# First norm's scale row spread by two products with ones, and another order of the first tiles, weights, mLSTM and FFN steps

## The chip, the cores and the metric

The kernel runs on one core of one Trainium2 chip. The metric is the time of one execution on the device, in microseconds (us). The profiler also records one execution: when each instruction began and how long it took on TensorE (PE, with PEld for its weight loads), VectorE (DVE), ScalarE (ACT), GpSimd (POOL) and SyncE (SP), what each waited for, what the 16 DMA engines moved, and the TensorE clock that was granted (1.00 is 2.4 GHz, 0.50 is 1.2 GHz).

## The reference

A trunk of two layers on 512 positions of width 1024, in float32. Layer 0 mixes with a chunked mLSTM, layer 1 with stick-breaking attention; each layer then cross-attends into 256 memory tokens and applies a SwiGLU FFN of inner width 2816. Every sub-layer is normalised before and after.

```
mem_n = rms_norm(mem, mem_norm_gain)
for layer in range(DEPTH):
    g = norm_gains[layer]
    hn = rms_norm(x, g[0])                        # g[0] of layer 0: the first norm's scale row
    y = mlstm_mixer(hn, ...) if layer % 2 == 0 else stick_breaking_mixer(hn, ...)
    x = x + rms_norm(y, g[1])
    y = memory_cross_attention(rms_norm(x, g[2]), mem_n, ...)
    x = x + rms_norm(y, g[3])
    y = swiglu_ffn(rms_norm(x, g[4]), ...)
    x = x + rms_norm(y, g[5])

# mlstm_mixer: proj = h @ w_in is split into q, k, v, output gate o and the head gates;
# per head scores with decay, hs = rms_norm(numerator / denominator), out = hs * sigmoid(o), out @ w_out
```

## The kernel before

**Numbers and products.** Each float32 operand of a product is kept as a high part (`hi`, rounded to fp32r) and a low part (`lo`, the rest). `split` makes them: a cast (`copy`, on ACT or DVE) and a subtraction on DVE. A product is three matmuls, lo·hi, hi·lo and hi·hi (`mm3` and `product`, issued at line 510). Transposes of activations (`flip`, line 524) also run on PE; four of them fill a bank of 512 columns.

**Weights** come in blocks of 128 x 1024 elements (512 KB), issued by SP (`dma`, line 418). Most projections use `seven` (line 643), which makes seven block products where eight would be needed: it loads three blocks, adds a fourth onto two of them with accumulating loads from POOL (`gather`, line 423), and forms its last sum `w10 + t2` on DVE, or with a third `gather` from SBUF to SBUF if its number in starting order is in `BY_DMA`.

**The start.** `warm` (line 770) runs 18 products of zeros on PE. SP loads the first 128 positions `xin[0]` in two halves, then the scale row of the first norm, broadcast to 128 partitions (`g0`, a 512 KB write), then by turns a pair of weight blocks for half of v (`w_tm`) and the next 128 positions. `arrive(t)` normalises tile t (sum of squares on ACT, logarithm and exponential on ACT, a few small steps on DVE, then one scaling by `g0` on DVE, line 468), flips it and splits it into `hi` and `lo`. The loop `for d in range(NT)` in `mlstm` brings tile d and weight d together and multiplies what has become possible. `constants` fills masks on POOL.

**mLSTM.** `MORDER` says in what order steps are made: `q`, `r` project q and k of two heads each, `+` is `sum_blocks` (sums of activation blocks that `seven` needs), `V` the other half of v, `s` scores, `h` heads, `o` and `P` the output gate. Then `proj_out` multiplies with `w_out` (eight blocks; here "out rows", three matmuls of 512 columns each per k), `boundary` does the norms, and `memory` normalises the 256 memory tokens and flips them.

**What sets the order.** Each operation is handed to `Plan.op` with an estimated duration and a rank (for PE the sum of PE time so far, moved by `later` and `sooner`). `lay_out` goes through time once and gives each engine, whenever it is free, the operation of least rank that can start and finds buffers; `LEAD` ranks the loads of some weights earlier, `SCARCE` keeps spare buffers from operations far ahead. The result is one fixed list for each engine, and every engine works its list strictly in order, so one late operation holds all behind it. Buffers are slots (44 of 4 KB and more, called `big`; 8 of 2 KB, `half`; 8 banks, `ps`).

Of the kernel before, what the change touches and what calls it, by code (L numbers as in the profile page):

```python
# [8 lines left out]
F32 = mybir.dt.float32  # L9
R = mybir.dt.float32r  # L10
# [6 lines left out]
P = 128  # L17
D = 1024
S = 512
NT = S // P  # L20
# [8 lines left out]
GROUPS = ((0, 8), (8, 16), (16, 22))  # L29
UNITS = ((0, '+', 2, 4, 6, 2, 6, 4, 2, 6, 8, 4, 8, (0, 1), (0, 0), 8, (0, 0), 10, (0, 0), (0, 1), 12, 14, 10, 14, (0, 1), 12, 10, 16, 14, 16, 12, 18, 16, 20, 18, 20, 20, (1, 0), (1, 1), (1, 1), 18, (1, 1), (1, 0), (1, 0)), (0, 2, 4, '+', 2, 6, 2, 4, 6, 8, 4, 6, (0, 1), 8, 8, (0, 0), (0, 1), (0, 0), (0, 1), (0, 0), 10, 10, 10, 12, 14, 16, 12, 18, 12, 14, 16, 14, 16, 18, 20, 20, 20, (1, 1), 18, (1, 0), (1, 0), (1, 1), (1, 0), (1, 1)))  # L30

# [346 lines left out]
class Trunk:  # L378
# [35 lines left out]

    def dma(self, eng, out, in_, ns=1400):
        q = {"SP": "sync", "POOL": "gpsimd", "ACT": "scalar"}[eng]
        cost = {"SP": 500, "POOL": 1040, "ACT": 60}[eng]
        self.plan.op(eng, cost, lambda nc: getattr(nc, q).dma_start(ap(out), ap(in_)), [in_], [out], load=ns)

# [65 lines left out]

    def memset(self, out, val):
        self.plan.op("POOL", 60 + 0.3 * out.free, lambda nc: nc.gpsimd.memset(ap(out), val), [], [out])

# [8 lines left out]

    def mms(self, items, **kw):

        ns, reads, writes = 0.0, [], []  # L500
# [11 lines left out]
        self.plan.op("PE", ns, fn, reads, writes)  # L512

# [250 lines left out]

    def gain(self, row, eng="POOL"):
        g = self.plan.buf("gain", (P, D))
        self.dma(eng, g, row.broadcast_to([P, D]))
        return g

    def warm(self, n):  # L770

        z, ps = self.half(S, dt=R), self.bank()
        self.memset(z.bitcast(F32), 0.0)
        self.mms([(ps, z[:, 0:P], z, True, True)] * n)
        self.plan.pe = 0.0

# [100 lines left out]
    def constants(self):  # L877
        self.eps = self.const(P, 1)
        self.memset(self.eps, EPS)
        raw = self.half(P)  # L880
# [4 lines left out]
        self.ident = self.ident_r.bitcast(F32)  # L885

        self.above = self.half(NT, P, dt=R)
        self.strict = self.const(P, 2, P, dt=R)
        for m, op, fill in ((self.above, ALU.is_ge, BIG), (self.strict, ALU.is_gt, -BIG)):
            raw = self.half(*m.idx.shape)  # L890
            self.memset(raw, 0.0)
# [4 lines left out]
        self.memset(raw, -1.0)  # L896
        self.select(raw[:, 0], ALU.is_ge, 0.0, 0, [[-1, P]], 1)
# [4 lines left out]
        raw = self.half(MLH, P)  # L902
        self.memset(raw, 0.0)
        for base in (0, -32):
# [5 lines left out]
    def mlstm(self, h, arrive, w_in, b_gate, head_gain, w_out, filler, finish):  # L910
        QK = MLH * MLK
# [11 lines left out]
        banks, ws = [], []  # L923
        for d in range(NT):
            with self.later(START * d):
                arrive(d)
                ws.append(self.w_tm(w_in, 2 * d, 2 * QK))
                banks.append(self.bank(2, 256))
                banks[d].buf.chained = True
                for t, u in [(t, d) for t in range(d)] + [(d, u) for u in range(d + 1)]:  # L930
# [3 lines left out]
        for t in range(NT):  # L934
            evac_v(0, t, banks[t])
        wg, bias = self.gate_weights(w_in[:, 2 * QK + 2 * D :], b_gate)
# [55 lines left out]

        hg = self.gain(head_gain)
        hs = [self.big(D) for _ in range(NT)]
# [544 lines left out]
def trunk_kernel(tc, x, mem, mem_norm_gain, norm_gains, ml_w_in, ml_b_gate, ml_head_gain, ml_w_out,  # L1539
# [117 lines left out]
```

## Time and profile before

| | |
|---|---|
| median of 3 runs | 1494.31 us (1491.07 to 1494.38) |
| the profiled execution | 1494.13 us, of which the span from first to last instruction is 1492.3 us |
| busy: PE, PEld, DVE, ACT, POOL | 1473.7, 1375.7, 1212.9, 863.2, 142.5 us |
| DMA | 191.00 MB, 128 GB/s over the span |
| granted TensorE clock, mean | 0.996 |

The span is nearly all PE time, so what counts is where PE stands still or runs below its usual pace. [...]

### The profile page before, as it was taken

Reading aid. Unit: us, or ns where it says so; the run is one execution under the profiler, and the core shown is the slowest. Engines: PE = TensorE matmul, PEld = TensorE weight load, DVE = VectorE, ACT = ScalarE, POOL = GpSimd, SP = SyncE. Lnnn points to the kernel's source line nnn. Section 1 sums busy time; section 2 is a strip of 40 time slices with the busy share of each in tenths; the row PEclk is TensorE's granted clock in tenths of the full one; section 3 lists DMA queues with packets and bytes.
Section 4 is the critical chain, followed back from the end, with each engine's and each line's share of the span. In section 5 each row is a group of like instructions: output and inputs, shape, how many; then the busy total and the mean of one; then the engine's idle time right before and its main releaser. Section 6 shows DMA issues by size and latency. Waiting matters only on the chain. (4 is left out here: it accounts for less than half of the span.)

```text
span 1492.3 us, 26099 instructions
## 1 busy us (share of the span) xinstructions
PE 1473.7 (99%) x10364; PEld 1375.7 (92%) x10364; DVE 1212.9 (81%) x1920; ACT 863.2 (58%) x1532; POOL 142.5 (10%) x180
## 2 busy tenths in 40 slices
PE   8999999999999999999999999999999999999998
PEld 6999889998999999998889888888988999999996
DVE  7979879886887786898868998879787969768985
ACT  7658655663654454654459896656556645444532
POOL 2100100100111111110100010001000111110110
PEclk9999999999999999999999999999999999999999
DMA  7446646532655566684400136244515563854651
GB/s 240 90 84 152 213 142 211 100 114 85 182 101 129 122 134 141 135 208 152 127 29 29 57 98 208 76 147 126 166 57 162 109 126 71 203 123 86 155 170 57
DMA packets 166955, 191.00 MB, mean 128 GB/s; under 512 B 6960, under 2 KB 140592, under 8 KB 166832
## 3 DMA queue, kind: packets, MB, share of 16 engines
q1 hardware_dynamic: 119776, 121.68, 25.5%
q0 software_dynamic: 47056, 67.64, 23.3%
q8 instruction: 82, 1.34, 0.4%
q14 instruction: 41, 0.34, 0.1%
HBM read 176.72 MB, written 10.49 MB: 125 GB/s over the span
## 5 line engine op out<-in xcount | busy, mean ns | idle before, releaser
L510 PE MATMUL ps<-big,big 128*128 128x256 f32 (+2 forms) x9712 | 1409.4, 306 | 7.4 <-ACT sm L434 2.7
L510 PEld LDWEIGHTS ps<-big,big 128*128 128x128 f32 x9712 | 1293.2, 189 | 91.5 <-ACT sm L434 2.9
L456 DVE TENSOR_TENSOR big<-big,big 128x1024 fp32r<-128x1024 f32 (+1 forms) x515 | 606.8, 1211 | 47.8 <-ACT big L441 27.4
L441 ACT CAST big<-big 128x1024 fp32r<-128x1024 f32 x388 | 393.4, 1044 | 154.8 <-DMA big<-in_ffn_w_gate_up_dram 48.2
L434 ACT ACTIVATE half<-ps 128x512 f32<-128x512 f32 (+4 forms) x185 | 92.7, 525 | 109.4 <-PE ps L510 100.0
L456 DVE TENSOR_TENSOR big<-ps,big 128x512 fp32r<-128x512 f32 (+3 forms) x188 | 109.5, 603 | 37.2 <-ACT big L441 23.9
L441 ACT CAST big<-ps 128x512 fp32r<-128x512 f32 (+2 forms) x166 | 81.4, 514 | 97.7 <-PE ps L510 61.2
L441 ACT COPY half<-ps 128x512 f32<-128x512 f32 (+2 forms) x102 | 59.6, 585 | 123.4 <-PE ps L510 116.1
L456 DVE TENSOR_TENSOR big<-half,big 128x512 fp32r<-128x512 f32 (+4 forms) x150 | 82.7, 577 | 7.2 <-ACT big L434 5.6
L434 ACT ACTIVATE half<-big 128x512 bf16<-128x512 f32 (+1 forms) x63 | 41.9, 666 | 72.6 <-DVE big L456 44.8
L423 POOL DMA_DIRECT2D big<-in_ffn_w_gate_up_dram x40 | 51.3, 1291 | 317.6 <-DVE big L456 193.1
L468 DVE SCALAR_TENSOR_TENSOR half<-ps,half 128x512 f32<-128x512 f32 (+2 forms) x74 | 46.8, 645 | 36.1 <-ACT half L441 20.9
L456 DVE TENSOR_TENSOR half<-ps,half 128x512 f32<-128x512 f32 (+2 forms) x78 | 46.8, 631 | 15.8 <-PE ps L510 14.3
L441 ACT CAST big<-half 128x512 fp32r<-128x512 f32 (+3 forms) x105 | 50.1, 521 | 13.4 <-DVE half L456 8.5
L456 DVE TENSOR_TENSOR big<-ps,gain 128x512 f32<-128x512 f32 x32 | 22.0, 687 | 35.6 <-ACT half L434 35.1
L434 ACT ACTIVATE half<-half 128x512 f32<-128x512 f32 (+2 forms) x74 | 40.5, 586 | 14.8 <-DVE half L456 14.5
L434 ACT ACTIVATE big<-ps 128x512 fp32r<-128x512 f32 (+2 forms) x66 | 38.4, 593 | 12.7 <-PE ps L510 9.3
L524 PE MATMUL ps<-const,big 128*128 128x128 f32 (+1 forms) x314 | 43.0, 275 | 2.0 <-DVE big L468 2.0
L524 PEld LDWEIGHTS ps<-const,big 128*128 128x128 f32 (+1 forms) x314 | 37.0, 143 | 7.8 <-issue 2.6
L510 PE MATMUL ps<-big,const 128*128 128x256 f32 (+3 forms) x224 | 41.0, 320 | 0.0
L510 PEld LDWEIGHTS ps<-big,const 128*128 128x128 f32 x224 | 36.4, 189 | 4.4
L461 DVE TENSOR_SCALAR sm<-sm,sm 128x1 f32<-128x1 f32 x99 | 23.8, 242 | 18.6 <-ACT half L434 10.0
(86 smaller groups left out, 616.0 us busy)
## 6 DMA issues: line engine op xcount, KB each, us to landing
big<-in_ffn_w_gate_up_dram SPq DMA_DIRECT2D x68, 512.0 KB, 5.2
big<-in_ffn_w_gate_up_dram POOLq DMA_DIRECT2D x40, 512.0 KB, 6.1
big<-in_ffn_w_down_dram SPq DMA_DIRECT2D x36, 512.0 KB, 5.8
big<-in_xa_w_kv_dram SPq DMA_DIRECT2D x32, 512.0 KB, 5.5
big<-in_sb_w_qkv_dram SPq DMA_DIRECT2D x24, 512.0 KB, 4.0
big<-in_ml_w_in_dram SPq DMA_DIRECT2D x19, 512.0 KB, 7.1
dr<-big POOLq DMA_DIRECT2D x16, 512.0 KB, 5.8
big<-in_xa_w_o_dram SPq DMA_DIRECT2D x16, 512.0 KB, 6.6
```

What stands on the lines that cost most here:

```text
L423: "POOL", 1040, lambda nc: nc.gpsimd.dma_start(ap(out), ap(in_), accum_op=ALU.add), [in_, out], [out], load=ns
L434: nc.scalar.activation(ap(out), ap(in_), func, scale=ap(scale), **kw)
L441: "ACT", 0.833 * n + (60 if psum else 95), lambda nc: nc.scalar.copy(ap(out), ap(in_)), [in_], [out],
L456: self._dve(out, [a, b], lambda nc: getattr(nc, q).tensor_tensor(out=ap(out), in0=ap(a), in1=ap(b), op=op), eng)
L461: nc.vector.tensor_scalar(out=ap(out), in0=ap(a), scalar1=ap(s1), scalar2=ap(s2), op0=op0, **kw)
L468: lambda nc: nc.vector.scalar_tensor_tensor(out=ap(out), in0=ap(a), scalar=ap(s), in1=ap(b), op0=op0, op1=op1),
L510: nc.tensor.matmul(ap(out), lhsT=ap(a), rhs=ap(b), start=start, stop=stop, **kw)
L524: nc.tensor.transpose(ap(out), ap(in_), ap(ident))
```

## The change

The scale row of the first norm is no longer loaded broadcast. `first_gain` loads the row once into one partition (from POOL), and two products with a row of ones spread it over 128 partitions; two copies bring it to `g0`. Zero products stand around them: 5 of 512 columns first, then 34 of 256 columns, which the planner may put wherever PE would wait. They are float32 products, unlike all others, where the row itself is multiplied. The order of the first tiles and weights becomes x, w, w, w, x, x, w, x. The masks are filled after the first v bank is done, and the mLSTM's head gain is loaded after all v banks. `MORDER` puts the first `q` ahead of `+`. `BY_DMA` changes; its number 39 is higher than any `seven` reaches, so q, V, r, P of the mLSTM and two of layer 0's FFN use the third gather, where before it was V, o, P and one of layer 0's FFN. Two FFN steps of layer 0 change places in `UNITS`, twice.

```diff
-MORDER = '+qqVqrsVVrrssosoohhPhhPP'
-START = 1250
+MORDER = 'q+VqqsrVVrrssosoohhPhhPP'
+START = 0
+SOON = 0
-BY_DMA = (1, 3, 4, 18)
+BY_DMA = (0, 1, 2, 4, 15, 20, 39)
-WARM = 18
+ARRIVE = 'xwwwxxwx'
+COLD, WARM = 5, 34
-LEAD = {'stick': 14000, 'ffn': 0, 'cross': 0, 'ml_out': 4500, 'sb_out': 2000, 'xa_out': 2000}
-SCARCE = {'ps': (4000, 0), 'big': (7000, 5), 'half': (4000, 2)}
+LEAD = {'stick': 14000, 'ffn': 0, 'cross': 0, 'ml_out': 3500, 'sb_out': 2000, 'xa_out': 2500}
+SCARCE = {'ps': (4000, 0), 'big': (7000, 5), 'half': (2000, 2)}
+    def first_gain(self, row):
+        src, ones, z, idle = self.big(D), self.half(P), self.half(S, dt=R), self.bank()
+        self.dma("POOL", src[0:1], row, 100)
+        self.memset(z.bitcast(F32), 0.0, "DVE")
+        self.memset(ones[0:1], 1.0, "DVE")
+        plan = self.plan
+        for _ in range(COLD):
+            self.mms([(idle, z[:, 0:P], z, True, True)], ns=430)
+            plan.pe = 0.0
+        g = self.plan.buf("gain", (P, D))
+        for c in (slice(0, 512), slice(512, D)):
+            ps = self.bank()
+            self.mms([(ps, ones[0:1], src[0:1, c], True, True)], ns=1300)
+            plan.pe = 0.0
+            self.copy(g[:, c], ps)
+        plan.pe = 0.0
+        with self.later(3000):
+            for _ in range(WARM):
+                self.mms([(idle[:, 0:256], z[:, 0:P], z[:, 0:256], True, True)])
+                plan.pe = 0.0
+        return g
-        for d in range(NT):
-            with self.later(START * d):
-                arrive(d)
-                ws.append(self.w_tm(w_in, 2 * d, 2 * QK))
+        for i, what in enumerate(ARRIVE):
+            with self.later(START * i), self.sooner(SOON * (len(ARRIVE) - 1 - i)):
+                if what == "x":
+                    arrive(len(banks))
+                else:
+                    ws.append(self.w_tm(w_in, 2 * len(ws), 2 * QK))
+        self.masks(banks[0])
-        hg = self.gain(head_gain)
+        hg = self.gain(head_gain, behind=banks)
-    k.warm(WARM)
+    g0 = k.first_gain(norm_gains[0, 0:1])
-    with k.sooner(3000):
-        g0 = k.gain(norm_gains[0, 0:1], "SP")
```

What the lists show at the places that matter. First SP, at the very start: `big_68` and `big_108` are the first two tiles of x before, `big_70` and `big_96` in the changed kernel; `in_ml_w_in` are weight blocks. Before:

```order
L418 DMA big_68<-in_x_dram 128x512 x2
L418 DMA gain_103<-in_norm_gains_dram 128x1024
L418 DMA big_106<-in_ml_w_in_dram 128x2x512
L418 DMA big_108<-in_x_dram 128x1024
L418 DMA big_111<-in_ml_w_in_dram 128x2x512
L418 DMA big_113<-in_x_dram 128x1024
```

and in the changed kernel:

```order
L422 DMA big_70<-in_x_dram 128x512 x2
L422 DMA big_80<-in_ml_w_in_dram 128x2x512
L422 DMA big_92<-in_ml_w_in_dram 128x2x512
L422 DMA big_96<-in_x_dram 128x1024
L422 DMA big_101<-in_ml_w_in_dram 128x2x512
L422 DMA big_108<-in_x_dram 128x1024
```

The broadcast scale row is gone from SP's list, and two weight blocks stand ahead of the second tile.

PE at the start before: `half_72` holds zeros, L524 are flips of a tile of x.

```order
L510 MATMUL ps_78<-half_72 128x512 x18
L524 MATMUL ps_166<-const_101,big_68 128x128 x4
L524 MATMUL ps_192<-const_101,big_68 128x128 x4
L510 MATMUL ps_235<-big_173,big_222 128x512
L510 MATMUL ps_235<-big_209,big_190 128x512
```

and in the changed kernel, where `half_68` holds zeros, `half_74` the ones, `big_72` the row:

```order
L516 MATMUL ps_76<-half_68 128x512 x5
L516 MATMUL ps_76<-half_68 128x256 x8
L516 MATMUL ps_117<-big_72,half_74 128x512
L516 MATMUL ps_156<-big_72,half_74 128x512
L516 MATMUL ps_76<-half_68 128x256 x10
L530 MATMUL ps_194<-const_98,big_70 128x128 x4
L516 MATMUL ps_76<-half_68 128x256 x12
L530 MATMUL ps_221<-const_98,big_70 128x128 x4
L516 MATMUL ps_76<-half_68 128x256
L516 MATMUL ps_231<-big_163,big_217 128x512
```

The two halves of the first tile are now flipped apart, and both, like everything behind, wait for the two products of the row. After these rows come, for the first tile, 11 more matmuls with w0 and w1, 3 zero products, 6 with w2, the flips of tile 1, 6 with w3, then tile 1's own.

ACT late in the mLSTM, where `P` waits for its last gathered block. Before (`big_1604` is that block, `ps_2084` a flipped piece of the heads, `sm_2119` the norm of the last heads):

```order
L441 CAST big_2071<-big_1881 128x1024
L434 ACTIVATE half_2089,sm_2006<-ps_2055 128x256
L441 CAST big_2108<-big_1604 128x1024
L434 ACTIVATE sm_2119<-sm_2112,const_66 128x4
L441 CAST big_2135<-ps_2084 128x2x128
L434 ACTIVATE sm_2119<-sm_2119 128x4
```

and in the changed kernel (`big_1613`, `ps_2113`, `sm_2148`):

```order
L438 ACTIVATE half_2118,sm_2035<-ps_2084 128x256
L445 CAST big_2135<-ps_2113 128x2x128
L445 CAST big_2139<-ps_2113 128x2x128
L438 ACTIVATE sm_2148<-sm_2141,const_66 128x4
L438 ACTIVATE sm_2148<-sm_2148 128x4
L445 CAST big_2165<-big_1613 128x1024
L445 CAST big_2171<-big_1918 128x1024
```

The cast of the gathered block now stands behind the norm of the last heads instead of ahead of it. On PE two more groups of four flips stand ahead of that block's product, and between it and the flips of the memory tokens there are 39 matmuls of 512 columns where there were 57. Behind the mLSTM's output projection PE's list is the same but for two small moves in layer 0's FFN and one in layer 1's cross-attention.

## Rows read from the trace of the kernel before

**Rows 1.** The page's first line.

```profile
span 1492.3 us, 26099 instructions
```

**Rows 2.** Busy time of each engine by stretch, granted clock, DMA share, GB/s.

```profile
4.50:9.00 4.50, 2.80 (x12) 1.95 (x11) 2.21 (x6) 2.19 (x6) 4.50 (x23) 1.00 0.98 315
11.30:18.10 6.80, 4.84 (x16) 4.09 (x17) 5.20 (x10) 5.96 (x14) 0.00 (x0) 0.50 1.07 375
60.00:160.00 100.00, 100.00 (x820) 98.95 (x819) 87.37 (x188) 70.69 (x155) 15.40 (x17) 1.00 0.53 115
160.00:166.00 6.00, 3.26 (x23) 2.83 (x22) 2.15 (x7) 3.23 (x7) 0.00 (x0) 0.91 1.06 388
200.00:620.00 420.00, 420.00 (x3140) 400.23 (x3139) 338.63 (x478) 231.61 (x378) 38.07 (x33) 1.00 0.53 129
```

**Rows 3.** Timeline of PE, first 23 us: start, length, count, idle before.

```profile
1.56 5.74 PE L510 MATMUL ps<-half 128*128 128x512 f32 x18 [1.56 <-POOL half L487]
9.30 1.23 PE L524 MATMUL ps<-const,big 128*128 128x128 f32 x8 [2.00 <-DVE big L468]
...
15.95 1.91 PE L524 MATMUL ps<-const,big 128*128 128x128 f32 x8
17.51 4.70 PE L510 MATMUL ps<-big,big 128*128 128x512 f32 x18
22.06 1.03 PE L524 MATMUL ps<-const,big 128*128 128x128 f32 x8
```

**Rows 4.** Timeline of DVE and ACT, first norm and first weight.

```profile
5.89 0.59 DVE L468 SCALAR_TENSOR_TENSOR sm<-sm,sm 128x1 f32<-128x1 f32 x1
...
7.95 1.87 DVE L468 SCALAR_TENSOR_TENSOR big<-big,sm,gain 128x512 f32<-128x512 f32 x2 [1.47 <-DMA gain<-in_norm_gains_dram]
...
9.28 1.05 ACT L441 CAST big<-big 128x1024 fp32r<-128x1024 f32 x1 [2.17 <-DMA big<-in_ml_w_in_dram]
```

**Rows 5.** DMA issues: count, KB each, median us from issue to landing.

```profile
big<-in_x_dram SPq DMA_DIRECT2D x2, 256.0 KB, 2.9
gain<-in_norm_gains_dram SPq DMA_DIRECT2D x1, 512.0 KB, 6.1
...
sm<-in_ml_b_gate_dram POOLq DMA_DIRECT2D x2, 0.0 KB, 7.0
```

**Rows 6.** Groups by shape, whole span: busy us, mean ns of one.

```profile
L456 DVE TENSOR_TENSOR big<-big,big 128x1024 fp32r<-128x1024 f32 x419 | 500.9, 1219 | 37.0 <-ACT big L441 26.8 <-PE ps L510 7.0 <-issue 1.1
...
L456 DVE TENSOR_TENSOR big<-ps,big 128x512 fp32r<-128x512 f32 x98 | 64.8, 685 | 16.5 <-ACT big L441 15.8
...
L468 DVE SCALAR_TENSOR_TENSOR big<-big,sm,gain 128x512 f32<-128x512 f32 x42 | 30.3, 759 | 2.1 <-DMA gain<-in_norm_gains_dram 1.5
...
L441 ACT CAST big<-big 128x1024 fp32r<-128x1024 f32 x382 | 389.8, 1050 | 154.4 <-DMA big<-in_ffn_w_gate_up_dram 48.2 <-DVE big L456 31.6 <-PE ps L510 28.6
...
L441 ACT CAST big<-ps 128x512 fp32r<-128x512 f32 x94 | 53.1, 589 | 70.6 <-PE ps L510 40.8 <-PE ps L524 24.8 <-issue 3.3
```

**Rows 7.** Timeline of SP, ACT and PE around the stop at 162 us.

```profile
142.56 15.42 SPq L418 DMA_DIRECT2D big<-in_ml_w_out_dram  x8
...
162.77 1.04 ACT L441 CAST big<-big 128x1024 fp32r<-128x1024 f32 x1 [3.82 <-DMA big<-in_ml_w_in_dram]
...
163.86 0.38 PE L510 MATMUL ps<-big,big 128*128 128x256 f32 x1 [1.86 <-ACT big L441]
165.12 4.42 PE L510 MATMUL ps<-big,big 128*128 128x256 f32 x23 [0.88 <-DVE big L456]
```

**Rows 8.** Timeline of DVE and PE at the flips of the memory tokens.

```profile
188.38 1.27 DVE L468 SCALAR_TENSOR_TENSOR big<-big,sm,gain 128x1024 f32<-128x1024 f32 x1
...
189.70 1.27 DVE L468 SCALAR_TENSOR_TENSOR big<-big,sm,gain 128x1024 f32<-128x1024 f32 x1
...
181.85 9.28 PE L510 MATMUL ps<-big,big 128*128 128x512 f32 x39
190.97 1.04 PE L524 MATMUL ps<-const,big 128*128 128x128 f32 x8
```

More of the change, by code (lines that the diff above doesn't have):

```diff
@@ L412, in sooner, with dma @@
         self.plan.lead = old
-    def dma(self, eng, out, in_, ns=1400):
+    def dma(self, eng, out, in_, ns=1400, behind=()):
         q = {"SP": "sync", "POOL": "gpsimd", "ACT": "scalar"}[eng]
         cost = {"SP": 500, "POOL": 1040, "ACT": 60}[eng]
-        self.plan.op(eng, cost, lambda nc: getattr(nc, q).dma_start(ap(out), ap(in_)), [in_], [out], load=ns)
+        self.plan.op(eng, cost, lambda nc: getattr(nc, q).dma_start(ap(out), ap(in_)), [in_, *behind], [out], load=ns)
     def gather(self, out, in_, ns=2800):
@@ L484, in vcopy, with memset @@
         self._dve(out, [a], lambda nc: nc.vector.tensor_copy(ap(out), ap(a)), fast=True)
-    def memset(self, out, val):
-        self.plan.op("POOL", 60 + 0.3 * out.free, lambda nc: nc.gpsimd.memset(ap(out), val), [], [out])
+    def memset(self, out, val, eng="POOL", behind=()):
+        q = {"DVE": "vector", "POOL": "gpsimd"}[eng]
+        self.plan.op(eng, 60 + 0.3 * out.free, lambda nc: getattr(nc, q).memset(ap(out), val), list(behind), [out])
     def select(self, out, op, fill, base, pattern, cm):
@@ L496, in select, with mms @@
         )
-    def mms(self, items, **kw):
-        ns, reads, writes = 0.0, [], []
+    def mms(self, items, ns=None, **kw):
+        given, ns, reads, writes = ns, 0.0, [], []
         for out, a, b, _, _ in items:
@@ L763, in rest, with gain @@
         return b[:, 0:1], b[:, 1:2]
-    def gain(self, row, eng="POOL"):
+    def gain(self, row, behind=()):
         g = self.plan.buf("gain", (P, D))
-        self.dma(eng, g, row.broadcast_to([P, D]))
+        self.dma("POOL", g, row.broadcast_to([P, D]), behind=behind)
         return g
[L770 to L775, printed above, removed]
+    def first_gain(self, row):
[19 more added lines that the diff above has]
+        return g
     def prenorm(self, out, x, g, steps=False):
@@ L885, in constants, with masks @@
         self.ident = self.ident_r.bitcast(F32)
+    def masks(self, behind):
         self.above = self.half(NT, P, dt=R)
@@ L890, in constants @@
             raw = self.half(*m.idx.shape)
-            self.memset(raw, 0.0)
+            self.memset(raw, 0.0, behind=[behind])
             self.select(raw, op, fill, 0, [[0, m.idx.shape[0]], [1, P]], -1)
@@ L895, in constants @@
         raw = self.half(2, P)
-        self.memset(raw, -1.0)
+        self.memset(raw, -1.0, behind=[behind])
         self.select(raw[:, 0], ALU.is_ge, 0.0, 0, [[-1, P]], 1)
@@ L902, in constants @@
         raw = self.half(MLH, P)
-        self.memset(raw, 0.0)
+        self.memset(raw, 0.0, behind=[behind])
         for base in (0, -32):
@@ L923, in mlstm @@
         banks, ws = [], []
[L924 to L930 removed]
+        for i, what in enumerate(ARRIVE):
+            with self.later(START * i), self.sooner(SOON * (len(ARRIVE) - 1 - i)):
+                if what == "x":
+                    arrive(len(banks))
+                    banks.append(self.bank(2, 256))
+                    banks[-1].buf.chained = True
+                    new = [(len(banks) - 1, u) for u in range(len(ws))]
+                else:
+                    ws.append(self.w_tm(w_in, 2 * len(ws), 2 * QK))
+                    new = [(t, len(ws) - 1) for t in range(len(banks))]
+                for t, u in new:
                     for k in (0, 1):
@@ L933, in mlstm @@
                         self.mm3(banks[t], h.tile(t, kk), ws[u][:, k], kk == 0, kk == KD - 1)
-        for t in range(NT):
-            evac_v(0, t, banks[t])
+                    if u == NT - 1:
+                        evac_v(0, t, banks[t])
+        self.masks(banks[0])
         wg, bias = self.gate_weights(w_in[:, 2 * QK + 2 * D :], b_gate)
```

4 lines of the change are left out of this document (2 added, 2 removed).

## The prediction

> **What bounds the kernel now.** I read the stretches first, then PE's timeline where PE stands still. The profiled execution took 1494.1 us, 1.8 more than its span [rows 1]; the median of the runs shown is 1494.3, so the sum below is made against 1494.1. From 60 to 160 us and from 200 to 620 us PE is busy in every microsecond at the full clock [rows 2], and 39 matmuls of 512 columns take 190.97 - 181.85 = 9.12 us there, 0.23 each [rows 8]. Such a stretch gets shorter only if PE has less to do, and the change takes nothing from its products. So I look for places where PE is not at that pace, and there are two that the change touches.
>
> The first is the start. The zeros end at 7.30, the first flips begin at 9.30, and only from 22.06, at the flips of the third tile, does PE run through [rows 3]. What it has done for the output by then is 16 flips and 24 matmuls (tiles 0 and 1 with weights 0 and 1): at 0.10 per flip (8 in the 0.8 us before the next matmuls, full clock) and 0.23 per matmul, 1.6 + 5.5 = 7.1 us. So 15 us are lost before 22.06, and no change of the start can bring more. The norm of the first tile is ready at 5.89 + 0.59 = 6.48, and DVE then waits 1.47 us for the scale row, which lands 6.1 us after its issue [rows 4, 5]. ACT waits 2.17 us for the first weight block, until 9.28 [rows 4]. In 11.3 to 18.1 the granted clock is half, after a stretch in which PE was mostly idle [rows 2].
>
> The second is a stop at 162 us. PE has nothing left at 162.0 (163.86 less 1.86 idle) and needs a gathered block of `P`, which ACT can cast only at 162.77; its low part releases PE at 165.12. PE stands idle for 1.86 + 0.88 = 2.7 us [rows 2, 7]. Eight blocks of `w_out`, issued by SP from 142.56 on, share the DMA engines with that gather (DMA share 1.06) [rows 2, 7].
>
> **The start, step by step.** Three things go: the 512 KB write of the broadcast row, the same for the head gain, and the wait for both on the way to the first weights. What comes: one row of 4 KB, two float32 products, two copies, zero products, and weights 0 and 1 ahead of tile 1. Let L be the time at which the row lands.
>
> Products. The trace has no float32 product of 512 columns. The nearest rows are the flips, 128 float32 columns each: 0.10 at the full clock (0.8 us for 8 before the next row), 0.20 at half (1.56 us for 8) [rows 3]. Four of these are 0.4 and 0.8. I take 0.8, as the clock at that time is just about to rise, and keep both. FP8 and Floating Point Precision, a page of the Trainium skill (TensorE Precision Notes), gives true float32 four passes; at the full clock that is an estimate of 0.85, the value I take.
>
> Chain, with 0.2 us from one engine to the next and the durations of the groups by shape [rows 6]:
> - PE: the row's products end at L+1.0 and L+1.8. DVE copies the first half (0.69) to L+1.9 and scales the first half tile (0.76) to L+2.7; flips at L+2.9.
> - ACT copies the second half (0.59) to L+2.6, casts w1 (1.05) to L+3.65, then the flipped half (0.59) to L+4.25. Weight 0 is cast before, while the row is on its way.
> - DVE: low part of w0 (1.22) L+3.9, second scaling L+4.65, low part of the flipped half (0.69) L+5.35, of w1 (1.22) L+6.6. PE: 12 matmuls from L+5.5 to L+8.3.
> - ACT: squares of tile 1, its logarithm and exponential, cast of w2, cast of the second flipped half: L+7.65. DVE: w2's low part, that half's (L+9.4), scaling of tile 1 (1.28, L+10.7). PE: 6 matmuls to L+11.0, flips of tile 1 to L+11.8.
> - ACT: two copies, squares of tile 2, cast of w3: L+11.15; DVE's low part L+12.4. PE: 6 matmuls to L+13.9.
>
> PE then has the work of 22.06 behind it and the next 24 matmuls before it, and their inputs come faster than it uses them. So the start ends at L+13.9 and breaks even at L = 8.2. With products of 0.4 it is L+13.1. The 34 zero products cost nothing on this path: at half of 0.23 each, 12 of them, 1.4 us, lie in the 1.5 us between the two groups of flips, and 10 in the copying and scaling. If their cover were gone they would cost 0.12 each.
>
> L: POOL issues the row at about 0.9. The nearest rows disagree: half a tile from SP, the first on empty engines, lands 2.9 us after its issue; two tiny loads from POOL, issued into a full queue (DMA share 0.98), took 7.0 [rows 2, 5]. So L lies between 3.8 and 7.9, and below 5 it does not help, since the norm is ready at 6.48 and the copy ends at L+1.9. I take 5.0, nearer to the empty engines, because nothing flows yet at 0.9. DMA: Bandwidth & Descriptors, of the Trainium skill (Anatomy of one DMA — SWDGE (gpsimd) path), gives a load from GpSimd about 2 us and its bytes' time: by that L is an estimate of 2.9, and the start would be bound by the norm alone. The trace does not agree for loads in company: 7.0 for a few bytes.
>
> The start then ends at 18.9 instead of 22.06: **-3.1 us**. Bounds: 7.9 + 13.9 = 21.8 gives -0.3; L at 5.0 with products of 0.4 gives 18.1, -4.0.
>
> **Masks, head gain, `q` before `+`.** DVE and ACT do the same masks later. From 22 us on PE did not wait although DVE was busy 87% to 160 [rows 2], and DVE now starts its work as much earlier as PE does, with two sums of 1.22 less (q and r by a third gather, o no more) and one copy more. I take nothing for these; uncovered, a sum would cost 1.2 us each.
>
> **The stop at 162.** For it, two groups of four flips (0.9 us) now stand ahead of the product that waits, and ACT does the last heads' norm ahead of the waiting cast. Against it, DVE is what PE meets next: from the gathered block to the memory tokens PE has 57 - 39 = 18 matmuls less between (4.2 us) and 0.9 of flips less, and DVE has five heads' steps, one low part and one weight's low part less, some 5 us. Before, the second scaling of memory tokens ended at 190.97, the moment at which PE came to them [rows 8]: no slack on PE's side. So what the stop loses, waits behind it give back. `w_out` loads: one more of the eight can be issued before the gather, so one fewer (512 KB, some 1.5 us) shares the engines with it. I take **0** here, with bounds of -2.7 (the stop is gone) and +3 (gather no earlier, and flips and memory tokens wait for DVE).
>
> **FFN and cross-attention.** Moves of one step where PE is busy at full pace [rows 2]: 0, and one `gather` for one sum of DVE.
>
> Sum: 1494.1 - 3.1 + 0 = **1491.0**.
>
> **Rivals.**
> (a) The stop at 162 closes: gather earlier by the load that is gone from its company, flips ahead. For it: the cast's wait of 3.82 us is a DMA wait alone [rows 7]. Against: DVE behind it. 1491.0 - 2.7 = 1488.3. Chance 0.24.
> (b) The row lands as late as the tiny loads: L = 7.9, 1493.8, and the change does at the start nothing that it says. For it: the row is a POOL load too, of 16 pieces. Against: empty engines. Chance 0.14.
> (c) The gather lands no earlier and DVE is late for the flips and the memory tokens: 1491.0 + 3 = 1494.0. Chance 0.12.
> (d) The other side: the clock falls during the start, as it did in 11.3 to 18.1 [rows 2]. PE then takes twice 0.23 per matmul for 24 of them: +5.5 where nothing hides it; 1491.0 + 5.5 = 1496.5, slower than before. It decides if PE stands idle for as large a share as before, that is if the row is so late that the 8 zeros before it are long done. Against: zeros now fill the waits in which it fell. Chance 0.08.
> (e) The row lands at once by the skill's figure, and products cost 0.4: -4.0, 1490.1. This is inside the forecast's own range, chance 0.1 of the forecast's.
>
> **Numbers.** Forecast with (e) 0.42, its own range 1489 to 1493. 0.3%, or 4.5 us, is about what a measurement of this kernel can tell from no change; so faster means under 1489.8, slower over 1498.8. Faster: (a) and a little of the forecast, where a small gain at 162 joins that of the start: 0.24 + 0.08 = 0.32. Slower: the bad ends of (d) and (c) together, 0.07. Same: 0.61. The range reaches from below (a), where it joins with L at its best, 1486.5, to above (d), 1497.
>
> **What the new profile would show.** Right: the row landing at 4 to 6 us; first flips at about 7.9; matmuls with real data from about 10.5; granted clock 1.00 from 5 us on; PE without a wait from 19 us. At the former 162 us, now some 3 us earlier, a shorter stop and after it waits of PE for DVE at flips or memory tokens. Wrong: a row that lands after 7 us, a product of the row over 1 us, a half clock in the first 20 us, or a wait in 20 to 60 us for q's third gather.

## The result, and the profile after

The changed kernel takes 1503.94 us (median of 5 runs, 1502.29 to 1509.2) against 1494.31 before: 1.0078 times, interval 1.0054 to 1.0102, 9.6 us slower. The forecast was 1491.0 with a range to 1497. The profiled execution took 1502.93 us, its span is 1501.2.

The stretches of the changed kernel, in the columns of [rows 2] (us, busy time of PE, PEld, DVE, ACT, POOL, granted clock, DMA share, GB/s):

```profile
4.50:9.00 4.50, 4.28 (x19) 2.86 (x19) 2.41 (x7) 2.70 (x7) 1.37 (x12) 0.89 1.00 361
60.00:160.00 100.00, 96.31 (x784) 94.57 (x784) 81.55 (x173) 69.29 (x152) 13.21 (x13) 1.00 0.53 112
160.00:166.00 6.00, 5.54 (x48) 5.33 (x48) 4.95 (x16) 3.03 (x8) 2.28 (x4) 1.00 1.12 307
200.00:620.00 420.00, 420.00 (x3125) 399.37 (x3124) 335.19 (x477) 226.32 (x370) 39.01 (x35) 1.00 0.53 130
680.00:692.00 12.00, 8.58 (x54) 8.18 (x54) 7.49 (x8) 6.84 (x7) 0.00 (x0) 0.86 0.60 201
```

From 60 to 160 us PE stood still for 3.7 us, where before it never did [rows 2]. From 200 to 620 PE is busy throughout in both. At 680 to 692 there is a hole that before did not have: 54 matmuls in 12 us, against 85 in the same stretch of before, and a clock of 0.86.

The timeline of PE in the start, against [rows 3] (start, length, count, idle before and who ended it):

```profile
1.54 3.77 PE L516 MATMUL ps<-half 128*128 128x512 f32 x13 [1.54 <-DVE half L493]
5.53 1.95 PE L516 MATMUL ps<-big,half 1*128 1x512 f32 x4 [0.22 <-DMA big<-in_norm_gains_dram]
7.41 2.01 PE L516 MATMUL ps<-half 128*128 128x256 f32 x10
9.22 1.05 PE L530 MATMUL ps<-const,big 128*128 128x128 f32 x4
9.92 2.37 PE L516 MATMUL ps<-half 128*128 128x256 f32 x12
12.13 0.60 PE L530 MATMUL ps<-const,big 128*128 128x128 f32 x4
...
12.68 2.94 PE L516 MATMUL ps<-big,big 128*128 128x512 f32 x12
```

The row's products run at 5.53, real matmuls from 12.68, and PE does not wait for over 0.3 us again before 35.8. To compare kernels whose programs differ, I counted the columns of all matmuls back from the last one: where the same number of columns is left, I took the difference of the two times. This difference is called the lag here, and a negative lag is a lead. By this the changed kernel leads by 2.2 us at 27 us, trails by 3.1 at 160, by 4.5 at 202 and by 3.5 at 654, and by 9.0 at 704; after that the difference stays. So the start gained, and two later stretches lost: 6.7 us from 27 to 202, in the mLSTM and what joins it, and 5.1 us (8.95 - 3.82, at 704.6 and 679.6) at 682 us.

The second loss, in the timelines of PE, ACT, SP and POOL of the changed kernel:

```profile
666.62 5.16 SPq L422 DMA_DIRECT2D big<-in_ffn_w_down_dram  x6
...
670.38 1.30 POOL L427 DMA_DIRECT2D big<-in_ffn_w_down_dram  x1 [5.12 <-DVE big L460]
671.16 1.62 POOL L422 DMA_DIRECT2D big<-dr  x2
...
682.04 5.79 ACT L445 CAST big<-big 128x1024 fp32r<-128x1024 f32 x6 [5.74 <-DMA big<-in_ffn_w_down_dram]
...
686.23 8.00 PE L516 MATMUL ps<-big,big 128*128 128x256 f32 x47 [3.42 <-DVE half L460]
```

At 670.38 POOL issues the last gather of layer 0's FFN (a gather is a load that adds a weight block onto another). Four down weights from SP (669.86 to 671.40) and two reloads of spilled rows (`big<-dr`) go out between 0.5 us before it and 1.3 us after, 512 KB each. ACT waits 5.74 us for the gather with the casts of weights that have landed queued behind it, DVE's low part follows, and PE starts 3.4 us late; then the granted clock is half from 687.3 to 690.7, which makes up the rest of the 5.1 us. The issue of that gather in the changed kernel, with KB and us to landing, and below it the same gather of before (at 663.89):

```profile
big<-in_ffn_w_down_dram POOLq DMA_DIRECT2D x1, 512.0 KB, 11.6
```

```profile
big<-in_ffn_w_down_dram POOLq DMA_DIRECT2D x1, 512.0 KB, 6.8
```

The mLSTM's stops in the changed kernel, timelines of ACT, PE and PE's weight loads:

```profile
100.27 1.05 ACT L445 CAST big<-big 128x1024 fp32r<-128x1024 f32 x1 [5.38 <-DMA big<-in_ml_w_in_dram]
...
102.72 1.55 PE L516 MATMUL ps<-big,big 128*128 128x256 f32 x11 [1.59 <-DVE big L460]
...
129.29 1.04 ACT L445 CAST big<-big 128x1024 fp32r<-128x1024 f32 x1 [3.73 <-DMA big<-in_ml_w_in_dram]
...
130.39 0.39 PE L516 MATMUL ps<-big,big 128*128 128x256 f32 x1 [1.19 <-ACT big L445]
131.65 2.44 PEld L516 LDWEIGHTS ps<-big,big 128*128 128x128 f32 x20 [1.07 <-DVE big L460]
...
166.54 3.89 ACT L445 CAST big<-big 128x1024 fp32r<-128x1024 f32 x4 [3.05 <-DMA big<-in_ml_w_in_dram]
...
174.67 5.93 PE L516 MATMUL ps<-big,big 128*128 128x256 f32 x48 [1.46 <-ACT half L445]
```

The first three ACT rows are the same picture: a gather lands late, ACT's cast waits for it, PE stops. At 174.67 PE waits for ACT, which was held by the third of these casts until 166.54 and fell behind with its other steps. The gather of 88.50 took 11.7 us beside a copy issued at 87.62 and two SP loads at 88.81 and 89.28; that of 119.99 took 9.3, that of 155.15 took 11.4 (10.8 before). The gather that before issued at 86.73, with nothing beside it, took 5.9, and even that was waited for, timeline of DVE in before:

```profile
92.77 0.69 DVE L442 CAST big<-big 128x1024 fp32r<-128x1024 f32 x1 [0.58 <-DMA big<-in_ml_w_in_dram]
```

### The profile page after: what moved, and what is told of

Same layout as the page of the kernel before. It is cut to its first block, busy times and chain, and to the rows that moved or that the text cites. A ratio compares the mean times of both kernels' runs of the same rounds, so it can differ in the third digit from the quotient of the medians.

```text
span 1501.2 us, 26153 instructions
## 1 busy us (share of the span) xinstructions
PE 1478.9 (99%) x10389; PEld 1379.2 (92%) x10389; DVE 1207.3 (80%) x1912; ACT 868.5 (58%) x1540; POOL 145.7 (10%) x182
## 5 line engine op out<-in xcount | busy, mean ns | idle before, releaser
L516 PE MATMUL ps<-big,big 128*128 128x256 f32 (+3 forms) x9712 | 1410.3, 305 | 12.3 <-DVE big L460 3.9
L460 DVE TENSOR_TENSOR big<-big,big 128x1024 fp32r<-128x1024 f32 (+2 forms) x513 | 605.0, 1210 | 60.9 <-ACT big L445 38.5
L445 ACT CAST big<-big 128x1024 fp32r<-128x1024 f32 (+1 forms) x392 | 397.0, 1044 | 153.3 <-DMA big<-in_ffn_w_gate_up_dram 37.9
L445 ACT COPY half<-ps 128x512 f32<-128x512 f32 (+1 forms) x104 | 60.9, 586 | 118.8 <-PE ps L516 110.4
L445 ACT CAST big<-half 128x512 fp32r<-128x512 f32 (+4 forms) x108 | 51.4, 516 | 19.1 <-DVE half L460 10.0
```

Of the source, the lines that this page charges most:

```text
L445: "ACT", 0.833 * n + (60 if psum else 95), lambda nc: nc.scalar.copy(ap(out), ap(in_)), [in_], [out],
L460: self._dve(out, [a, b], lambda nc: getattr(nc, q).tensor_tensor(out=ap(out), in0=ap(a), in1=ap(b), op=op), eng)
```

## The experiments

Each line of this table is a kernel: its median, that of before measured beside it, and its lag behind before in the profiled executions at equal work left (negative: ahead), by the times of the variant in us. Where the order of steps differs from that of before, a lag is good to about 0.5 us in the start and 1 us inside the mLSTM. stop_zeros has no figure where the products that it adds later would have to be taken out.

| kernel | us | before | 27 | 160 | 202 | 654 | 704 |
|---|---|---|---|---|---|---|---|
| changed kernel | 1503.94 | 1494.31 | -2.2 | 3.1 | 4.5 | 3.5 | 9.0 |
| a_bydma | 1498.68 | 1493.57 | -2.6 | 2.0 | 4.8 | 4.6 | 4.6 |
| a_mlstm_dma | 1504.57 | 1493.57 | -2.7 | 2.0 | 5.0 | 4.9 | 10.3 |
| a_ffn_dma | 1500.38 | 1493.57 | 0.2 | 8.7 | 9.8 | 8.4 | 8.5 |
| a_start | 1495.15 | 1493.57 | 0.2 | 4.1 | 2.7 | 2.1 | 2.1 |
| b_order | 1497.04 | 1493.77 | -2.4 | 3.6 | 3.9 | 3.8 | 3.7 |
| b_lead | 1497.73 | 1493.77 | -2.4 | 1.3 | 4.3 | 3.7 | 3.6 |
| row_full | 1494.20 | 1493.77 | -0.8 | 1.5 | 1.2 | 0.7 | 0.7 |
| b_zeros | 1492.97 | 1493.77 | -0.4 | 0.0 | 1.4 | 0.9 | 1.0 |
| no_20 | 1504.35 | 1493.49 | -2.7 | 4.0 | 6.4 | 5.5 | 9.2 |
| no_15 | 1504.58 | 1493.49 | -2.8 | 3.9 | 6.3 | 5.4 | 10.5 |
| hg_free | 1495.92 | 1493.49 | -1.9 | 2.8 | 2.5 | 2.1 | 2.1 |
| row_full2 | 1495.42 | 1493.49 | -0.8 | 1.5 | 1.2 | 1.6 | 1.6 |
| ffn_none | 1502.40 | 1494.11 | -3.1 | 2.6 | 4.7 | 3.9 | 7.4 |
| ffn_18_20 | 1499.34 | 1494.11 | -2.6 | 4.2 | 5.0 | 4.1 | 4.5 |
| tables | 1505.72 | 1494.11 | -0.6 | 5.6 | 7.4 | 6.2 | 11.4 |
| stop_zeros | 1493.80 | 1494.11 | | | -0.5 | -0.7 | -0.7 |
| row_only | 1500.12 | 1492.56 | -2.5 | 6.8 | 7.6 | 6.9 | 7.0 |
| arrive_only | 1494.96 | 1492.56 | -0.1 | 1.7 | 1.3 | 0.9 | 0.9 |

Two figures quoted in the expectations below come out otherwise by this count: at 27 us a_start is 0.2 behind before, not 1.4, and a_bydma 2.6 ahead, not 3.1.

Some of these kernels run the same lists for a long way, and show how far two profiles of one program lie apart. The changed kernel, a_ffn_dma, no_20, no_15, ffn_none and ffn_18_20 have the same tiles in the same order on every engine until 545 us; their lags at 202 are 4.5 to 6.4, and 9.8 in a_ffn_dma, whose start ran longer at half clock. a_start and b_lead are alike until 176 us, and lie 2.8 apart at 160. So a difference of 2 us between two single profiles shows nothing by itself; a stop that comes in all profiles of one list does. The changed kernel's three stops between 100 and 176 us do: in the six profiles the gather ahead of the first takes 11.7 to 12.2 us, that ahead of the second 9.0 to 9.3.

Theory at first: sums moved to the DMA make weight loads late, at 682 us and in the mLSTM. Rival: the order of steps and the planner's reserves do it.

**a_bydma.**

```diff
-BY_DMA = (0, 1, 2, 4, 15, 20, 39)
+BY_DMA = (1, 3, 4, 18)
```

> The kernel after, with BY_DMA as before (1, 3, 4, 18) and all else as changed. Theory (copies by DMA make weight loads late): TensorE's stop of 3.6 us at 682 us and the 1.5 us that half clock costs behind it go, and so do the stops at 101 us (1.75) and 129 us (2.5); 1494 to 1497 us, 7 to 10 below after. Rival (the order of steps and the reserves do it, the copies are incidental): the stops stay, within 2 us of after, about 1503.

The stop at 682 is gone; in the mLSTM other stops came, at 60, 66, 91, 140 and 180 us, where PE waits for steps of DVE and ACT (of gates and heads at 61 and 141) and not for a gather, and the lag at 202 is the same (4.8 against 4.5). The theory holds for the FFN alone, and the median of 1498.68 lies above the range that it gave. The stops at 60 and 140 in PE's timeline:

```profile
61.29 1.63 PE L516 MATMUL ps<-half,const 128*128 128x512 f32 x6 [0.82 <-DVE half L460]
...
141.39 0.86 PE L516 MATMUL ps<-big,big 128*128 128x256 f32 x5 [1.19 <-DVE big L472]
```

**a_mlstm_dma.** `BY_DMA = (1, 3, 4, 15, 20, 39)`

> The kernel after, with the mLSTM's sums by DMA as before (V, o and P, not q, V, r and P), the FFN's as changed. Theory: the stops at 101 and 129 us go, 3 to 5 us below after (1499 to 1501), and the stop at 682 us stays at 3 to 4 us with half clock behind it. Rival (order of the steps): the mLSTM's stops stay, about 1503.

The stops at 101 and 129 went, as expected, and those of a_bydma came in their place: nothing won.

**a_ffn_dma.** `BY_DMA = (0, 1, 2, 4, 18)`

> The kernel after, with layer 0's FFN sum by DMA as before (number 18 alone, not 15 and 20), the mLSTM's as changed, and the changed order of units kept. Theory: SyncE's six loads of down weights no longer wait 25.5 us for the copy of rows (1, 1), the stop at 682 us and the half clock go, 5.1 us below after (1498 to 1499.5); the stops before 200 us stay as they are. Rival (the order 12, 16, 18 of the units does it): the stop stays, about 1503.

By the medians 3.6 us below the changed kernel, and no stop at 682, though the changed order of units is kept. But in its profile the start was 0.2 us behind before, where the other profiles of this program led by 2.2 to 3.1, for a reason that a_start shares.

**a_start.** The start as changed; these lines as before:

```diff
-MORDER = 'q+VqqsrVVrrssosoohhPhhPP'
+MORDER = '+qqVqrsVVrrssosoohhPhhPP'
-BY_DMA = (0, 1, 2, 4, 15, 20, 39)
+BY_DMA = (1, 3, 4, 18)
-LEAD = {..., 'ml_out': 3500, 'sb_out': 2000, 'xa_out': 2500}
+LEAD = {..., 'ml_out': 4500, 'sb_out': 2000, 'xa_out': 2000}
-SCARCE = {..., 'half': (2000, 2)}
+SCARCE = {..., 'half': (4000, 2)}
```

and `UNITS` of before.

> The kernel after, with BY_DMA, the order of the mLSTM's and the FFN's steps, LEAD and SCARCE all as before: the start alone is changed (row by two products with ones, order of arrivals, zero products, masks and head gain held back). Theory (the start gains the 2.2 us by which after leads at 27 us, and it is given back later only by the other parts): 1491.5 to 1493 us, 1.5 to 3 below before. Rival (whatever the start gains is given back by the stop at 162 us, since the load that it waits for comes no earlier): 1494 to 1495.

Both were off: 1.6 us above before. PE's timeline in the start of a_start, then of a_bydma, whose program is the same there:

```profile
1.53 4.21 PE L516 MATMUL ps<-half 128*128 128x512 f32 x13 [1.53 <-DVE half L493]
5.67 3.78 PE L516 MATMUL ps<-big,half 1*128 1x512 f32 x4
...
12.39 2.45 PE L516 MATMUL ps<-half 128*128 128x256 f32 x12
14.67 0.60 PE L530 MATMUL ps<-const,big 128*128 128x128 f32 x4
```

```profile
5.67 2.02 PE L516 MATMUL ps<-big,half 1*128 1x512 f32 x4
...
9.27 1.67 PE L516 MATMUL ps<-half 128*128 128x256 f32 x12
10.78 0.60 PE L530 MATMUL ps<-const,big 128*128 128x128 f32 x4
```

In a_start the clock was half until 14.1 us: the row's products took 3.7 us instead of 1.9, and the second flips came at 14.67 instead of 10.78. PE had done the same until then, zeros from 1.53 and then products that use one row of the array. Among the thirteen profiles with these products at 5.3 to 5.9 us the clock was full by 6.4 us and stayed up in five, fell behind the products in six, and rose only at 13 to 14 us in two. The difference stays: a_bydma is 3.9 us ahead of a_start at 14 us and 2.9 from 20 to 40 us, b_lead 2.8 us ahead at 28 us and 2.9 at 70.

**b_order.** a_start with the changed `MORDER`.

> The kernel a_start (start as changed, all tables as before) with the changed order of the mLSTM's steps, q+VqqsrVV for +qqVqrsVV. a_bydma, with this order and the changed reserves, went from 3.1 us ahead of before at 27 us to 4.8 behind at 202; a_start lost 1.4 in the same stretch. Theory (the order of the steps loses it): 5 to 7 us above a_start, 1500 to 1502, with stops of TensorE near 60, 66, 140 and 180 us. Rival (LEAD and SCARCE do it): within 1 us of a_start, about 1495.

**b_lead.** a_start with the changed `LEAD` and `SCARCE`.

> The kernel a_start with the changed LEAD and SCARCE, order of steps and sums by DMA as before. Theory (the order of the steps loses the time, not the reserves): within 1 us of a_start, about 1495. Rival (the reserves lose it): 5 us above, about 1500.

They stand 1.9 and 2.6 us above a_start, so neither theory nor rival holds alone. From 27 to 160 us b_order lost 6.0 us, a_start 3.9 and b_lead, with the same lists as a_start, 3.7 (a_bydma and a_mlstm_dma, with the order of b_order until 69 us at least, 4.6 and 4.7): there the order of the steps costs some 1 to 2 us, no more than repeats differ by, and the reserves nothing. What the reserves bring comes behind 176 us, a stop of 1.5 us at 181. In the profiles b_lead also ran at half clock from 165.6 to 172.4 and a_start did not, so their lags at 202, 4.3 and 2.7, show more than the edit.

**row_full.** a_start with the row's products over 128 rows, the same sums:

```diff
+        self.memset(src, 0.0, "DVE")
...
-        self.memset(ones[0:1], 1.0, "DVE")
+        self.memset(ones, 1.0, "DVE")
...
-            self.mms([(ps, ones[0:1], src[0:1, c], True, True)], ns=1300)
+            self.mms([(ps, ones, src[:, c], True, True)], ns=1300)
```

> The kernel a_start, in which the products of the row go over 128 rows (ones over all 128, the row's buffer zeroed but for the row; the same sums) in place of one. In a_start's profile TensorE stood at half clock until 14.1 us, in that of a_bydma at full from 5.8 on, with the same program until then; a_start was 1.4 behind before at 27 us, a_bydma 3.1 ahead. Theory (products that use one row of the array are what the clock is not raised on, or falls behind): full clock from 4 to 7 us on in the profile, the four records of the two products within 2.5 us, 1491 to 1493, below a_start by 2 to 4. Rival (the clock comes as it falls, whatever the products use): as a_start, 1494.5 to 1495.5.

**row_full2.** The same, with the zeros' buffer cleared by GpSimd (`self.memset(z.bitcast(F32), 0.0)`).

> The kernel row_full with its zero products' buffer cleared by GpSimd, so that they begin before 2 us and not at 2.6. row_full's profile stood at full clock from 7.3 us on and its products of the row took 2.1 us at that clock, but it began a microsecond later than a_start. Theory (with products over 128 rows the clock stays up, and a start 1 us earlier is worth that): 1492.5 to 1493.8, below before by 0 to 1; the clock full from 4 to 8 us on and never half in the start. Rival (the clock's fall depends on when it comes, not on the rows): 1494 to 1495.5, with a half clock between 5 and 14 us as in after.

In both profiles the clock rose at 7.3 and 6.0 us and did not fall in the start. That speaks for the theory, but two profiles do not show it, and it does not pay: the row comes later (5.6 us from issue to landing in row_full, 3.5 in a_start), and the medians are 0.4 and 1.9 above before, the first 1 us below a_start, the second level with it.

**b_zeros.** Before, with the zero products of the waits alone:

```diff
         self.mms([(ps, z[:, 0:P], z, True, True)] * n)
         self.plan.pe = 0.0
+        with self.later(3000):
+            for _ in range(34):
+                self.mms([(ps[:, 0:256], z[:, 0:P], z[:, 0:256], True, True)])
+                self.plan.pe = 0.0
```

> The kernel before, with the 34 zero products of 256 columns put into the waits of its first products and nothing else changed. Theory (the half clock from 11.3 to 18.1 us of before costs what its products take longer, some 1.5 to 3 us, and zeros in the gap keep it up): 1490.5 to 1492, full clock from 5 to 20 us. Rival (before waits for weights and rows in that stretch whatever the clock, so that the stretch ends no earlier): 1493 to 1494.5.

The stretch that stood at half clock in [rows 2]:

```profile
11.30:18.10 6.80, 5.49 (x37) 4.55 (x36) 6.00 (x10) 5.99 (x14) 0.52 (x1) 1.00 1.07 373
```

Full clock, and yet only 0.4 us ahead at 27 us: in the profile the rival is right, that stretch waits for rows and weights. The median lies between the two ranges. At 0.9992 (0.9983 to 1.0000) it is the fastest kernel here, by less than one can tell.

**hg_free.** a_start with `hg = self.gain(head_gain)`, not held back.

> The kernel a_start, in which the head gain's 512 KB are not held back behind the first matmuls. In a_start it is issued at 43.7 us, 0.8 us behind the third gather of q, which then takes 7.0 us from issue to landing and not 6.0, and TensorE stops for 1.08 us at 50.8. Theory (the two transfers share the queue and the 16 engines): that stop goes or falls under 0.3 us, 0.5 to 1.5 us below a_start, 1493.7 to 1494.7, unless the gain now delays the row or the first weights. Rival (VectorE and ScalarE, not the gather, are what that product waits for): the stop stays, about 1495, or the first real products come later by the 1.3 us that 512 KB take, 1496.

The theory fell: the gain is out of the way, the gather took 7.8 us all the same, with no other transfer in flight, the stop is 1.0 us, and the median is no lower than that of a_start. Why that gather was slow is open.

**no_20** (`BY_DMA = (0, 1, 2, 4, 15)`) and **no_15** (`BY_DMA = (0, 1, 2, 4, 20)`).

> The kernel after, in which of layer 0's FFN sums by DMA number 20, rows (1, 1), is added by VectorE again; number 15 (pair 14) stays with the DMA. Theory (the copy of rows (1, 1), issued at 656.7 us and landed at 664.2, holds the buffer for which SyncE's queue waits, and six down weights come late): no stop of TensorE at 682 us, no half clock after it, SyncE's last six loads of down weights before 660 us; 3.5 to 5 us below after, as a_ffn_dma, 1499 to 1500.5. Rival (pair 14, or both): the stop stays, 1503 to 1504.5.

> The kernel after, in which number 15 (pair 14) is added by VectorE again and number 20, rows (1, 1), stays with the DMA. Theory (the copy of rows (1, 1) alone): the stop at 682 us stays, 3 to 4 us, as after, 1503 to 1504.5. Rival (pair 14 has a part in it): a shorter stop, 1499 to 1501.

Numbers are in starting order: 15 belongs to the weights that `UNITS` calls pair 14, 18 to pair 20, 20 to rows (1, 1). A copy here is the third gather, from SBUF to SBUF. Without the copy of rows (1, 1) a stop of 1.9 us is left, without that of pair 14 all of it, 3.5. The copy of rows (1, 1) explains 1.5 of 3.4 us; what a_ffn_dma had besides was the sum of pair 20 on the DMA. Neither median is below that of the changed kernel, so the theory of no_20 missed.

**ffn_none** (`BY_DMA = (0, 1, 2, 4)`) and **ffn_18_20** (`BY_DMA = (0, 1, 2, 4, 18, 20)`).

> The kernel after with no FFN sum of layer 0 by DMA (neither 15, 18 nor 20), the mLSTM's as changed. Theory 1 (the stop at 682 us is there whenever pair 20's third block, number 18, is added by VectorE, since the loads behind it are then issued in one bunch with the gather): the stop stays at 2 us or more, 1502 to 1505. Theory 2 (copies of 15 and 20 by DMA make the bunch): no stop, 1498 to 1501.

> The kernel after with numbers 18 and 20 of layer 0's FFN by DMA and not 15. Theory 1 (pair 20's copy by DMA keeps the loads apart): no stop at 682 us, or under 1 us, 1498 to 1501.5. Theory 2 (the copy of rows (1, 1), number 20, holds back SyncE's queue): a stop of 2 us or more and the half clock behind it, 1502 to 1505.

Both medians lie where theory 1 put them. The timeline of PE in ffn_none, then that of SP, POOL and PE in ffn_18_20:

```profile
684.67 7.51 PE L516 MATMUL ps<-big,big 128*128 128x256 f32 x43 [1.79 <-DVE half L460]
```

```profile
662.45 12.72 SPq L422 DMA_DIRECT2D big<-in_ffn_w_down_dram  x6
...
671.90 1.30 POOL L427 DMA_DIRECT2D big<-in_ffn_w_down_dram  x1 [4.74 <-DVE big L460]
672.67 1.08 POOL L422 DMA_DIRECT2D big<-dr  x1
...
679.75 12.50 PE L516 MATMUL ps<-big,big 128*128 128x256 f32 x96
```

With pair 20's sum on the DMA three other transfers of 512 KB go out within 2 us of the last gather, which takes 6.6 us; without it (ffn_none) five do, and it takes 10.0. Taken together, with the changed order of units in all: number 18 on the DMA gives no stop, with or without 20; without 18 the stop is 1.8 us, 1.9 with 15, 3.5 with 20, and 3.4 with both.

**tables.** Before, with the changed `MORDER`, `UNITS`, `BY_DMA`, `LEAD` and `SCARCE`, its start unchanged.

> The kernel before, its start unchanged (broadcast row, 18 zero products, masks and head gain early), with all changed tables: order of the mLSTM's and the FFN's steps, sums by DMA, LEAD and SCARCE. If the start and the tables add up (a_start was 1.6 above before), 1501.5 to 1503; stop at 682 us of 3.5 us with the half clock, and 3 to 6 us lost between 27 and 200. Rival (the tables fit only the changed start, or lose only with it): 1496 to 1499 or above 1505.

11.6 above before: the tables alone lose as much as the whole change. By the medians it is 2 us more, as the changed start would give back; but the ratios, 1.0076 (1.0060 to 1.0092) and 1.0078 (1.0054 to 1.0102), do not tell them apart.

**row_only** (before with `first_gain` in place of `warm` and of the broadcast) and **arrive_only** (before with the changed loop over `ARRIVE`).

> The kernel before with the scale row spread by products and with the zero products, and nothing else of the change: arrival order, masks, head gain and tables as before. Theory (the row gives the gain, the later stops come from the other parts of the start): 2 to 3 us ahead of before at 27 us where the clock is full by 6 us, no stop of over 0.5 us between 40 and 160 us, 1491 to 1492.5. Rival (any move in the start shifts the loads behind it, so stops come with the row too): 1493.5 to 1496.

> The kernel before with the changed order of arrivals alone (weights 0 to 2 between tiles 0 and 1), its broadcast row and 18 zero products kept. Theory (the order makes no later stop and gains nothing by itself, since TensorE waits for the row): 1493 to 1495. Rival (the order makes the stops at 51 and 61 us, 1 us each): 1495 to 1497.

arrive_only lies in its theory's range, with 0.1 us gained at 27 us and one stop of 0.7 at 134. row_only is far above both of its ranges: it leads by 2.5 us at 27 and 2.6 at 52 us, and then loses 10. ACT and PE of row_only:

```profile
54.03 1.04 ACT L441 CAST big<-big 128x1024 fp32r<-128x1024 f32 x1 [5.26 <-DMA big<-in_ml_w_in_dram]
54.98 0.58 ACT L441 COPY half<-ps 128x512 f32<-128x512 f32 x1
55.46 0.61 ACT L441 CAST half<-half 4x512 fp32r<-4x512 f32 x1
55.98 0.62 ACT L434 ACTIVATE half<-half 4x512 f32<-4x512 f32 x1
...
56.66 0.41 PE L526 MATMUL ps<-const,half 4*128 4x4 f32 x4 [2.72 <-ACT half L434]
```

The gather of 45.59 took 8.4 us beside two SP loads; ACT's queue stood behind its cast, and with it the gates' small steps that PE needed. Further stops follow at 130, 145 and 169 us, and half clock came behind this one and those at 130 and 169. Nothing was edited there: the planner places each step by the times that it reckons for earlier ones, so an edit of the start redraws the mLSTM: the lists of PE, ACT and DVE there are no longer those of before.

**stop_zeros.** b_zeros with 16 zero products ahead of the product that waits at 162 us, added to the bank in use:

```diff
         self.gather(t3, src(1, 0))
+        if number == 4:
+            z = self.half(256, dt=R)
+            self.memset(z.bitcast(F32), 0.0)
+            for _ in range(16):
+                self.mms([(v[:, 1], z[:, 0:P], z, False, False)], skip_group_check=True)
```

> The kernel b_zeros (before with 34 zero products in its start) with 16 more zero products of 256 columns, 1.9 us, ahead of the product for which TensorE waits at 162 us (they add zeros to the bank that is being summed). Theory (after the stop TensorE runs at half clock for 3.4 to 6.8 us in all profiles but a_start's, which costs 1.7 to 3.4): no half clock between 160 and 175 us, 1490.5 to 1492, 1 to 3 below before. Rival (the clock falls all the same, or the zeros come ahead of work that was not waiting): 1493 to 1495.

```profile
160.04 2.06 PE L510 MATMUL ps<-half 128*128 128x256 f32 x16
162.98 0.38 PE L510 MATMUL ps<-big,big 128*128 128x256 f32 x1 [0.88 <-ACT big L441]
164.24 4.28 PE L510 MATMUL ps<-big,big 128*128 128x256 f32 x23 [0.88 <-DVE big L456]
```

The zeros ran in the wait, and the clock still fell to half, from 165.5 to 168.9: the rival, and the median is level with before. The last 1.8 us of the stop are not covered.

## Why the prediction was wrong

- **The start, -3.1: right in kind.** The row landed at 5.4 (issued at 1.38, 4.0 us on the way) where 5.0 was taken, each product took 0.94 us (7.41 less 5.53, halved) where 0.8 was, first flips came at 9.22 and not 7.9, real matmuls at 12.68 and not 10.5. The gain is 2.2 us in the profile, with half clock from 8.1 to 11.5. The Trainium skill's four passes for float32 (FP8 and Floating Point Precision, TensorE Precision Notes) gave 0.85 us for a product, an estimate; the trace agrees within 0.1. Rival (d), a half clock, came in eight of thirteen profiles with these products: over zeros and flips it cost little (the lead at 27 us is 1.9 to 2.8 us where it fell, 2.4 to 3.1 where it stayed up), but where it rose only at 14 us it cost 2.9 us at 27 us (0.2 behind in a_start, 2.6 ahead in a_bydma), about half of the 5.5 forecast.
- **Masks, head gain, q before +: 0. This step failed.** It read from [rows 2] that PE never waited from 60 to 160 us and concluded that moves there are free. But a stretch without a wait was not one with room. In before the gathers of that stretch took 5.9 to 8.1 us and ACT waited for none, though one landed just in time (that of 86.73, for which DVE waits 0.6 us); in the changed kernel two took 11.7 and 9.3, ACT, which casts them in order, waited 5.4 and 3.7, and PE stopped. Between 27 and 160 us, for which the prediction put nothing, the changed kernel lost 5.3 us, 3.7 of them in stops of PE; the six profiles of its list lost 5.3 to 8.5. Which edit does it is not one: the order, the start and even the row alone bring stops here, the reserves one at 181, in other places each time, and not all at gathers (a_bydma). The head gain is not it (hg_free lost 4.7 in the same stretch); the masks were not tried by themselves.
- **The stop at 162, 0: too low, but inside its bounds.** From 160 to 202 us the lag grew by 1.4 us. The gather took 11.4 us from issue to landing (10.8 before), ACT waited 3.05 (3.82), and half clock came behind it as before. Flips ahead of it only moved the wait. Rival (a) did not happen. Of rival (c) half came: the gather was no quicker, flips waited 0.5 us for DVE, and a product at 174.67 waited 1.5 us for ACT; the memory tokens did not wait. Of the signs named against the forecast two came, the half clock of the start and a wait in 20 to 60 us, of 0.4 us at 36.2.
- **FFN, "one gather for one sum of DVE": 0. This step failed, by 5.1 us.** Counting DVE's time misses what the copy does to the order of loads: with number 18 off the DMA, five or six other transfers of 512 KB go out within 2 us of the last gather, which takes 10.0 to 11.8 us; with it on, two or three do and the gather takes 6.6 to 7.8. Number 18 off costs a stop of 1.8 us, number 20 on another 1.6, and half clock behind it the rest.
- **The sum**, -3.1, came out as -2.2 + 5.3 + 1.4 - 1.0 + 5.4 = 8.9 at 704 us (the start, the mLSTM, the stretch at 162, a little won back to 654, and the FFN). It took the profile of before, whose plan has no stop from 22 to 160 us, as if it would be kept. Of the 18 kernels of the experiments only b_zeros and stop_zeros, which leave tables and loads alone, have no stop of over 0.5 us between 20 and 160 us.

Still open: by which of its rules the planner bunches the loads. The runs show that in the changed kernel PE stops where gathers land late, not why each plan issues them so; in a_bydma the stops at 61 and 141 us are waits for small steps of DVE. For the FFN the cause is shown by the six settings of numbers 15, 18 and 20. For the mLSTM it is argued from the timelines: no experiment there parts two transfers with all else kept.

## What to carry to other kernels

A stretch in which the bound engine never waits is not a stretch with slack: look at how late its transfers land and how late the other engines' steps end, and price each load that is moved or bunched, not only the engine time of what it replaces. Where a planner orders the program, an edit of one place changes all later ones: measure the gain at the edit and at the end apart, by work left, and set two profiles of one program side by side first, to see how far they differ with no edit at all. A gain of 2 to 3 us that is real at 27 us was lost three times over by 200.

## What the hardware showed that was not expected

- How long a gather of 512 KB takes goes with how many other transfers of that size are issued within 2 us of it. Over the 1480 gathers of the 20 profiles the median is 6.0 us with none, 6.4 with one, 7.3 with two and 10.1 with three, and none of the 24 with four or more took under 10.0. The spread is wide: with two it is 5.6 to 10.5, and with nothing else in flight 5.6 to 7.8. The Trainium skill's fit for a load from GpSimd (DMA: Bandwidth & Descriptors, Anatomy of one DMA — SWDGE (gpsimd) path), worked out for 512 KB, is an estimate of 3.2 us; it does not say that it holds for a load that adds, and no gather here was that fast.
- A stop can cost more than itself: half clock behind the one at 682 us took another 1.7 us (5.1 less 3.4), and behind the one near 162 us it came in all 20 profiles but a_start's, also where 16 zero products filled the first 2 us of the stop.
- The same first instructions got full clock at 5.8 us in one profile and at 14.1 in another, 2.9 us apart at 27 us; the lists behind the start did not take such a lead away (b_lead against a_start: 2.8 us at 28, 2.9 at 70, 2.8 at 160).
